# Two-layer fp32 backbone: weights, rows and accumulators moved to 0 modulo 512 bytes of SBUF

## The chip, the cores and the metric

The kernel runs on one core of a Trainium2 chip. The metric is the device time of one execution in microseconds (us). Below, PE is the matmul engine, PEld its weight loads (they run beside its matmuls), DVE the vector engine, ACT the scalar engine, POOL GpSimd and SP the engine that issues the DMAs.

## The reference

Two layers of a trunk work on 256 latent tokens and 256 context tokens, with D = 2048 and a hidden width of F = 5504, all in fp32. Layer 0 mixes tokens by pooling, on both streams. In layer 1 the latent tokens attend to a neighbourhood and to all context tokens (32 heads of 64), and the context is no longer written. A gated FFN with a width-3 convolution over tokens follows each mixer. The shift, scale and gate vectors of a layer come from `silu(c) @ w_mod`.

```python
def conv_ffn(u, w_gate, w_up, conv_w, conv_b, w_down):
    gp = jnp.pad(u @ w_gate, ((0, 0), (1, 1), (0, 0)))
    gte = gp[:, :T] * conv_w[0] + gp[:, 1:T + 1] * conv_w[1] + gp[:, 2:] * conv_w[2] + conv_b
    return (jax.nn.silu(gte) * (u @ w_up)) @ w_down
...
for i in range(DEPTH):
    ml = (silu_c @ w_mod[i] + b_mod[i]).reshape(B, 6, 1, D)
    mc = (silu_cc @ w_mod[i] + b_mod[i]).reshape(6, 1, 1, D)
    a_lat = modulate(rms_norm(h, norm1_g[i]), ml[:, 0], ml[:, 1])
    a_ctx = modulate(rms_norm(hc, norm1_g[i]), mc[0], mc[1])
    ... # y_lat, y_ctx: pool_mix in layer 0, neighbourhood_attention in layer 1
    h = h + ml[:, 2] * y_lat
    h = h + ml[:, 5] * conv_ffn(modulate(rms_norm(h, norm2_g[i]), ml[:, 3], ml[:, 4]), ...)
    if not last:
        hc = hc + mc[2] * y_ctx
        hc = hc + mc[5] * conv_ffn(modulate(rms_norm(hc, norm2_g[i]), mc[3], mc[4]), ...)
return rms_norm(h, final_norm_g)
```

## The kernel before

Activations are kept transposed: D runs over 16 tiles (KT) of 128 partitions, tokens along the free axis. `hl` and `hc` hold the two residual streams. A matmul streams token rows (the moving operand, 512 columns at a time) past a 128 by 128 weight block. Every fp32 operand is split into a high part, rounded to the fp32r format by a CAST on ACT, and a low part, the rest, subtracted on DVE. A product is then three matmuls: high by high, high by low, low by high. In layer 0 the 512 columns are the two streams side by side, and each k-tile takes the three matmuls in turn (`gu_mm`, L912 to L914, and `down0`, L949 to L951). In layer 1 high and low rows of the latent stream lie side by side, so that one matmul of 512 columns makes the first two products and one of 256 columns the third: eight of the one, then eight of the other (`gu_b`, L1102 and L1109; the o projection, L1466 and L1470), or four and four (`down1`, L1174 and L1178).

Weights arrive by SP's DMA queue as tiles of 128 x 1024 fp32 in the pool `wst` (4096 bytes per partition). `split` (L138) turns each tile, a half of a weight panel, into high and low tiles. It takes their buffers from a rotating list: the pool `whp` (three pairs) alone in most stages; in layer 0's FFN three turns of `whp` and one of `whx`; in layer 1's FFN three of `whp` and five of `whx1`. The normed rows lie in `ap0` (`A` in layer 0 and the projections, `oA` in layer 1), the activated hidden rows in the tiles `act` of the pool `f0` (layer 0) and `actb` of `f1` (layer 1).

Stages follow one another in the order norm and modulation, the pooling mixer with the first parts of the gate and up products (F-tiles 0 to 7), layer 0's FFN (`gu0(f)` for the gate and up products of F-tile f, `down0` once for every four F-tiles), attention, the o projection, layer 1's FFN (`gu1`, `down1`). The modulation for layer 1 is folded in among layer 0's FFN, on DVE and PE (L260, L282, `modt_b` at L320), and its sums are spread into `modT` (L330). `down0` evicts a PSUM bank on ACT (`dy`, L967) and adds it to `hl` and `hc` on POOL (L970).

SBUF tiles are placed by pools: a pool is opened where the last one ends, and the tiles of a pool stand in the order of their first mention, one address for all 128 partitions. A pool that is closed gives its space to the next ones, and an instruction on a new tile waits for what last used that space. A scheduler that is part of the build then puts the instructions of each engine in order by its own estimate of when each can run; so what a tile has to wait for can move an instruction. The pools `main`, `wst`, `whp` and `ap0` stay open throughout. Because `main` begins with the vector table `vt` of 3744 bytes, all that comes after it stands at other residues.

Residues modulo 512 bytes in the program as built, before: `wst`, `whp`, `ap0` and `hc` 192; `f0` (with `act`), `whx`, the modulation's sums and `whx1` 320; `f1` 192, with `actb` in it at 320; the attention's pools 448; `hl` 480.

Of the kernel before, what the change touches and what calls it, by code (L numbers as in the profile page):

```python
# [10 lines left out]
F32 = mybir.dt.float32  # L11
F32R = mybir.dt.float32r
# [5 lines left out]
P = 128  # L18
D = 2048
KT = D // P  # L20
T = 256
# [7 lines left out]
NK = BAND + T  # L29
# [3 lines left out]
NS = 8  # L33
# [27 lines left out]
def kernel(ctx: ExitStack, tc: tile.TileContext, xT, cxT, wmod, wg, wu, wd, wp,  # L61
                         wq, wv, wo, vec, cc, rope, inv, strips, out):
    nc = tc.nc
    main = ctx.enter_context(tc.tile_pool(name="main", bufs=1))
# [16 lines left out]
        return a.rearrange("p s t -> p (s t)")  # L81


    vt = main.tile([P, NVEC], F32, name="vt")
    nc.sync.dma_start(vt, vec)

# [1 line left out]
        a, b = _OFF[name]  # L88
        return vt[:, a:b]

    ones = main.tile([P, 1], F32, name="ones")
    nc.gpsimd.memset(ones, 1.0)
    minus_half = main.tile([P, 4], F32, name="minus_half")
    nc.gpsimd.memset(minus_half, -0.5)
    ident = main.tile([P, P], F32, name="ident")
    make_identity(nc, ident)

    sc2 = main.tile([P, KT, 2], F32, name="sc2")
    nc.sync.dma_start(sc2, cc)
    nc.scalar.activation(sc2, sc2, AF.Silu)  # L100
    hl = main.tile([P, KT, T], F32, name="hl")


    extra = []
# [367 lines left out]
    with ExitStack() as ph0:  # L472
        p0 = ph0.enter_context(tc.tile_pool(name="p0", bufs=1, reuse_waits="tile"))
# [9 lines left out]
            return f0.tile([P, 2, 512], dt, tag="act", bufs=7, name=name)  # L483

        PART = {}
        wsh = p0.tile([P, 2, NS, 2], F32, name="wsh")

        def late(f):

# [41 lines left out]

        with ExitStack() as phs:
            st = phs.enter_context(tc.tile_pool(name="st", bufs=2, reuse_waits="tile"))
            sc = st.tile([P, 32 * KT + 30], F32, bufs=1, name="sc")
            nc.gpsimd.memset(sc, 0.0)
            nc.vector.tensor_copy(sc[:, 30:].rearrange("p (k c) -> p k c", c=32)[:, :, 0:2], sc2)
# [7 lines left out]
                if 3 <= k < 13:  # L544
                    nc.tensor.matmul(warm[:, :T], ident, sq[:, :T], start=True, stop=True)
            pr = n1.rstd()
            rs1 = st.tile([P, 512], F32, bufs=1, name="rs1")
            nc.scalar.copy(rs1, pr)
            n2 = Norm(both, p0, "n2")
            n2.acc = p0.tile([P, 512], F32, name="n2acc")  # L550
# [4 lines left out]
            for j in range(2):  # L555
                t = st.tile([P, 2, WP], F32, bufs=1, name=f"pad{j}")
# [3 lines left out]
            for j in range(2):  # L560
                t = st.tile([P, 158], F32, bufs=1, name=f"sh{j}")
# [451 lines left out]
    for _ in moves:  # L1013
        pass
    tail, rows = _attention(tc, ap0, bank, ld, A, M, hl, wq, wv, wo, rope, band, ident, v_first)

    with ExitStack() as ph2:
        f1 = ph2.enter_context(tc.tile_pool(name="f1", bufs=8, reuse_waits="tile"))
# [11 lines left out]
        for k in range(KT):  # L1030
            a = raw[k] = rows[k][:, 1]
            with n4.urgent(k):
                nc.scalar.activation(a[:, 0], hl[:, k, :], AF.Copy, scale=M(1, 4, k, 0))
                nc.vector.scalar_tensor_tensor(a[:, 1], hl[:, k, :], M(1, 4, k, 0), a[:, 0].bitcast(F32),
                                               op0=ALU.mult, op1=ALU.subtract)
        sh = f1.tile([P, KT, 2], F32R, bufs=1, name="sh")
        for k in range(0, KT, 4):
            v = modT[1, 12 + k // 4][:, :, 0]
            nc.scalar.copy(sh[:, k : k + 4, 0], v)
# [215 lines left out]
def _attention(tc, ap0, bank, ld, A, M, hl, wq, wv, wo, rope, band, ident, v_first):  # L1255
# [9 lines left out]
    with ExitStack() as es:  # L1265
        op = es.enter_context(tc.tile_pool(name="op", bufs=1, reuse_waits="tile"))
        at = es.enter_context(tc.tile_pool(name="at", bufs=2, reuse_waits="tile"))
        rp = op.tile([P, 2, T], F32, name="rp")
        raw = at.tile([P, 2, T], F32, tag="sb", bufs=3, name="rope_rows")
        nc.sync.dma_start(raw, rope)  # L1270
# [2 lines left out]

        sts = []
        for j in range(2):
            t = op.tile([P, NK], F32, name=f"bias{j}")
            nc.gpsimd.memset(t, 0.0)
            sts.append(t)

        pts = []  # L1280
        for j in range(2):
            t = op.tile([P, 4, T], F32, name=f"pt{j}")
# [4 lines left out]
        for j in range(2):  # L1287
            t = op.tile([P, 2, T], F32R, name=f"qz{j}")
# [318 lines left out]
```

## Time and profile before

| | us |
|---|---|
| median of 3 runs | 3028.66 (3026.96 to 3032.0) |
| profiled execution, span | 3027.4 |
| layer 0's FFN, window 408 to 1664 | 1256.00 |
| attention up to the o projection, window 1664 to 2180 | 516.00 |
| layer 1's FFN, window 2289 to 3007 | 718.00 |

The profile is of one execution, and its span is 1.3 us below the median. A row of a window gives its length, then the busy time of each engine and the number of instructions in it, then the granted PE clock, the busy share of the DMA engines and what they moved. The durations that the profile gives to a matmul run to its end, which overlaps the next one; the time that a matmul costs in a row of many is the distance from start to start.

### The profile page before, as it was taken

How to read it: one execution, taken by the hardware profiler on the slowest of the kernel's cores; microseconds unless marked ns; L12 is line 12 of the kernel's file. 1: busy time of each engine (PE TensorE's matmuls, PEld its weight loads, DVE VectorE, ACT ScalarE, POOL GpSimd, SP SyncE). 2: the span in 40 equal slices, each digit the busy share in tenths (PEclk: the TensorE clock that was granted, in tenths of full speed). 3: DMA queues.
4: the chain of work that ended last, by engine and by line, in shares of the span. 5: the costliest groups of instructions: out<-in, count | busy, mean ns of one | idle time of the engine just before them, and what ended most of it. 6: DMA issues, size and time to landing. Idle time of an engine off the chain costs nothing.

```text
span 3027.4 us, 41070 instructions
## 1 busy us (share of the span) xinstructions
PE 2975.9 (98%) x14922; PEld 2405.5 (79%) x14922; DVE 2031.5 (67%) x2908; ACT 1353.1 (45%) x2225; POOL 872.1 (29%) x864
## 2 busy tenths in 40 slices
PE   7999999999999999999999999999999999999998
PEld 3655678887888888888887888888888888888887
DVE  4455887666776867687676666474777666666666
ACT  3333573323334233333334444343556666566665
POOL 1011310302214030332413111110101565566665
PEclk9999999999999999999999999999999999999999
DMA  9988535455865867786783333333356555555553
GB/s 380 342 299 324 197 99 179 159 170 167 251 201 186 257 178 234 210 234 200 216 241 101 115 108 114 99 110 108 112 162 206 175 196 194 188 182 188 182 187 112
DMA packets 224923, 572.32 MB, mean 189 GB/s; under 512 B 55248, under 2 KB 68304, under 8 KB 224720
## 3 DMA queue, kind: packets, MB, share of 16 engines
q1 hardware_dynamic: 224720, 569.70, 58.5%
q8 instruction: 117, 1.92, 0.3%
q14 instruction: 86, 0.70, 0.1%
HBM read 563.32 MB, written 11.53 MB: 190 GB/s over the span
## 4 chain that ended last, share of the span: by engine, by line
PE 89%; DVE 5%; DMA 2%; issue 1%; ACT 1%; SPq 0%; POOL 0%; POOLq 0%; DVEq 0%; ACTq 0%
PE u L1102 5%; PE g L1102 5%; PE d L1174 5%; PE d L949 5%; PE d L951 5%; PE d L950 5%; PE u L914 4%; PE u L912 4%; PE u L913 4%; PE g L914 4%; PE g L913 4%; PE g L912 4%; PE u L1109 3%; PE g L1109 3%; PE d L1178 3%; PE mod L195 2%
## 5 line engine op out<-in xcount | busy, mean ns | idle before, releaser
L970 POOL TENSOR_TENSOR hl<-hl,dy 128x256 f32<-128x256 f32 x144 | 145.1, 1008 | 943.4 <-ACT dy L967 678.4
L1191 POOL TENSOR_TENSOR hl<-hl,dy 128x256 f32<-128x256 f32 x320 | 313.5, 1011 | 234.4 <-ACT dy L1189 231.4
L282 DVE SCALAR_TENSOR_TENSOR macc<-wm,sc,macc 128x512 f32<-128x512 f32 x360 | 263.2, 780 | 8.1 <-DMA wm<-wmod 7.8
L260 DVE SCALAR_TENSOR_TENSOR macc<-wm,sc,macc 128x1024 f32<-128x1024 f32 x120 | 160.7, 1339 | 95.7 <-DMA wm<-wmod 94.5
L967 ACT ACTIVATE dy<-d,modT 128x256 f32<-128x256 f32 x224 | 93.2, 470 | 133.2 <-PE d L951 129.1
L970 POOL TENSOR_TENSOR hc<-hc,dy 128x256 f32<-128x256 f32 x144 | 141.9, 986 | 0.0
L1189 ACT ACTIVATE dy<-d,modT 128x512 f32<-128x512 f32 x160 | 104.5, 684 | 57.5 <-PE d L1178 57.2
L1371 POOL COPY bias<-rows 128x160 f32<-128x160 f32 x64 | 39.6, 628 | 311.6 <-DVE nm L1380 228.3
L153 DVE TENSOR_TENSOR wd_3l<-wd,wd_3h 128x1024 fp32r<-128x1024 f32 (+1 forms) x44 | 56.0, 1277 | 79.9 <-ACT wd_3h L150 79.9
L195 PE MATMUL mod<-wm,sc 128*32 128x512 f32 x640 | 96.5, 607 | 5.7 <-DMA wm<-wmod 5.5
L516 ACT ACTIVATE sg<-g 128x512 f32<-128x512 f32 x43 | 27.3, 634 | 153.2 <-DVE g L513 153.1
L153 DVE TENSOR_TENSOR wd_2l<-wd,wd_2h 128x1024 fp32r<-128x1024 f32 (+1 forms) x44 | 58.8, 1347 | 46.1 <-ACT wd_2h L150 46.1
L606 POOL TENSOR_TENSOR pf<-ws,inv 128x256 f32<-128x256 f32 x32 | 28.6, 914 | 196.6 <-DVE ws L598 137.6
L153 DVE TENSOR_TENSOR wd_1l<-wd,wd_1h 128x1024 fp32r<-128x1024 f32 (+1 forms) x44 | 55.3, 1260 | 37.7 <-ACT wd_1h L150 37.7
L150 ACT CAST wd_0h<-wd 128x1024 fp32r<-128x1024 f32 (+1 forms) x44 | 45.1, 1030 | 61.5 <-PE g L913 49.0
L150 ACT CAST wd_1h<-wd 128x1024 fp32r<-128x1024 f32 (+1 forms) x44 | 44.9, 1026 | 56.3 <-PE u L1102 29.6
L949 PE MATMUL d<-act,wd_0h 128*128 128x512 f32 x172 | 67.4, 395 | 1.0 <-ACT dy L967 1.0
L949 PE MATMUL d<-act,wd_3h 128*128 128x512 f32 x172 | 68.2, 396 | 0.0
L950 PE MATMUL d<-act,wd_2h 128*128 128x512 f32 x172 | 68.1, 396 | 0.0
L951 PE MATMUL d<-act,wd_1l 128*128 128x512 f32 x172 | 67.7, 394 | 0.2 <-DVE wd_1l L153 0.2
L951 PE MATMUL d<-act,wd_0l 128*128 128x512 f32 x172 | 67.9, 395 | 0.0
L949 PE MATMUL d<-act,wd_1h 128*128 128x512 f32 x172 | 67.9, 395 | 0.0
(1710 smaller groups left out, 9327.3 us busy)
## 6 DMA issues: line engine op xcount, KB each, us to landing
wm<-wmod SPq DMA_DIRECT2D x384, 512.0 KB, 6.2
wd<-wd SPq DMA_DIRECT2D x168, 512.0 KB, 4.4
wg<-wg SPq DMA_DIRECT2D x156, 512.0 KB, 4.4
wu<-wu SPq DMA_DIRECT2D x156, 512.0 KB, 4.7
wv<-wv SPq DMA_DIRECT2D x32, 512.0 KB, 3.9
wk<-wq SPq DMA_DIRECT2D x32, 512.0 KB, 3.9
wq<-wq SPq DMA_DIRECT2D x32, 512.0 KB, 3.7
wo<-wo SPq DMA_DIRECT2D x32, 512.0 KB, 4.4
```

Source lines behind the costliest of these rows:

```text
L153: low = eng.tensor_tensor(lo[:, :n], t[:, :n], hi[:, :n].bitcast(F32), op=ALU.subtract)
L282: nc.vector.scalar_tensor_tensor(acc[:, s], w, sc2[:, k, s : s + 1], acc[:, s], op0=ALU.mult, op1=ALU.add)
L912: nc.tensor.matmul(ps, hi[:, c : c + P], xh, start=(k == 0), stop=False)
L913: nc.tensor.matmul(ps, hi[:, c : c + P], xl, start=False, stop=False)
L914: nc.tensor.matmul(ps, lo[:, c : c + P], xh, start=False, stop=(k == KT - 1))
L949: nc.tensor.matmul(ps, hi[:, o : o + P], xh, start=(i == 0), stop=False)
L950: nc.tensor.matmul(ps, hi[:, o : o + P], xl, start=False, stop=False)
L951: nc.tensor.matmul(ps, lo[:, o : o + P], xh, start=False, stop=(i == n - 1))
L970: nc.gpsimd.tensor_tensor(h_of(s)[:, k, :], h_of(s)[:, k, :], y[:, s], op=ALU.add)
L1102: ins = nc.tensor.matmul(ps, hi[:, c : c + P], flat(x[k]), start=(k == 0), stop=False)
L1109: nc.tensor.matmul(ps[:, T:], lo[:, c : c + P], x[k][:, 0], start=False, stop=(k == KT - 1))
L1191: nc.gpsimd.tensor_tensor(hl[:, k, :], hl[:, k, :], y[:, q], op=ALU.add)
```

## The change

No operation, size or loop is changed, only where tiles stand. In `main`, `wsh` and `sh` come from other pools to the front, `sc2`, `ident` and `hl` ahead of `vt`, and `ones` is made 24 floats wide. In the pool `st`, `rs1` stands ahead of `sc`. The attention's two `bias` tiles go to a pool of their own, `odd`, opened behind the others.

```diff
@@ main pool
+    wsh = main.tile([P, 2, NS, 2], F32, name="wsh")
+    sh = main.tile([P, KT, 2], F32R, name="sh")
+    sc2 = main.tile([P, KT, 2], F32, name="sc2")
+    ident = main.tile([P, P], F32, name="ident")
+    hl = main.tile([P, KT, T], F32, name="hl")
     vt = main.tile([P, NVEC], F32, name="vt")
     nc.sync.dma_start(vt, vec)
...
-    ones = main.tile([P, 1], F32, name="ones")
+    ones = main.tile([P, 24], F32, name="ones")[:, 0:1]
     nc.gpsimd.memset(ones, 1.0)
     minus_half = main.tile([P, 4], F32, name="minus_half")
     nc.gpsimd.memset(minus_half, -0.5)
-    ident = main.tile([P, P], F32, name="ident")
     make_identity(nc, ident)
 
-    sc2 = main.tile([P, KT, 2], F32, name="sc2")
     nc.sync.dma_start(sc2, cc)
     nc.scalar.activation(sc2, sc2, AF.Silu)
-    hl = main.tile([P, KT, T], F32, name="hl")
@@ layer 0
         PART = {}
-        wsh = p0.tile([P, 2, NS, 2], F32, name="wsh")
...
             st = phs.enter_context(tc.tile_pool(name="st", bufs=2, reuse_waits="tile"))
+            rs1 = st.tile([P, 512], F32, bufs=1, name="rs1")
             sc = st.tile([P, 32 * KT + 30], F32, bufs=1, name="sc")
...
             pr = n1.rstd()
-            rs1 = st.tile([P, 512], F32, bufs=1, name="rs1")
             nc.scalar.copy(rs1, pr)
@@ layer 1
-        sh = f1.tile([P, KT, 2], F32R, bufs=1, name="sh")
         for k in range(0, KT, 4):
             v = modT[1, 12 + k // 4][:, :, 0]
             nc.scalar.copy(sh[:, k : k + 4, 0], v)
@@ attention
         op = es.enter_context(tc.tile_pool(name="op", bufs=1, reuse_waits="tile"))
         at = es.enter_context(tc.tile_pool(name="at", bufs=2, reuse_waits="tile"))
+        odd = es.enter_context(tc.tile_pool(name="odd", bufs=1, reuse_waits="tile"))
         rp = op.tile([P, 2, T], F32, name="rp")
...
-            t = op.tile([P, NK], F32, name=f"bias{j}")
+            t = odd.tile([P, NK], F32, name=f"bias{j}")
             nc.gpsimd.memset(t, 0.0)
             sts.append(t)
```

In the changed program as built, `wst`, `whp`, `ap0`, `hc`, `f0`, `act`, `whx`, the modulation's sums, `f1`, `actb`, `whx1`, `hl` and `ident` stand at 0 modulo 512, the attention's tiles at 0 and its score rows at 0 and 128, `vt` at 0, `sc2` and the second `bias` tile at 384. Every engine keeps its number of instructions, and lines stand one or two lower. `sh` and `bias` are in space that is free earlier, which moves a few instructions.

On POOL, before, behind the last adds of `down0` (`hl` and `hc` take `dy`, the first number being the output tile) and the norm (`n3v`), the two MEMSETs of `bias`:

```order
L970 TENSOR_TENSOR hl<-hl,dy_15_12756 128x256
L970 TENSOR_TENSOR hc<-hc,dy_15_12756 128x256
L388 TENSOR_TENSOR n3v_13076<-n3v_13076,minus_half 128x2
L388 TENSOR_TENSOR n3v_13080<-n3v_13080,minus_half 128x2
L1277 MEMSET bias_13478 128x416
L1277 MEMSET bias_13480 128x416
L1283 MEMSET pt_13482 128x1024
L1283 MEMSET pt_13484 128x1024
```

On POOL in the changed program, in the last but one pass of `down0`:

```order
L971 TENSOR_TENSOR hl<-hl,dy_11_12649 128x256
L971 TENSOR_TENSOR hc<-hc,dy_11_12649 128x256
L971 TENSOR_TENSOR hl<-hl,dy_12_12703 128x256
L971 TENSOR_TENSOR hc<-hc,dy_12_12703 128x256
L1278 MEMSET bias_13482 128x416
L1278 MEMSET bias_13484 128x416
L971 TENSOR_TENSOR hl<-hl,dy_13_12721 128x256
L971 TENSOR_TENSOR hc<-hc,dy_13_12721 128x256
L971 TENSOR_TENSOR hl<-hl,dy_14_12739 128x256
L971 TENSOR_TENSOR hc<-hc,dy_14_12739 128x256
```

The MEMSETs have moved up past the residual adds of three output tiles and past the norm.

On ACT, before, between attention and the o projection (`O` and `oA` are attention's output and its split, `wo3h` a cast weight):

```order
L1383 ACTIVATE sb_1_17920,sm_1_17923<-sb_1_17920,nm_1_17921 128x416
L1409 COPY O_17948<-o_17939 128x256
L1453 CAST oA_17957<-O_17948 128x256
L1039 CAST sh<-modT_86 128x4 x4
L150 CAST wo3h_18019<-wo_0_18015 128x1024
L150 CAST wo3h_18023<-wo_1024_18017 128x1024
```

On ACT in the changed program, in the last but one pass of `down0`:

```order
L152 CAST wd_10_0h_12770<-wd_10_0_1024_12764 128x512
L968 ACTIVATE dy_11_12649<-d_9_2_3_12636,modT_87 128x256 x2
L968 ACTIVATE dy_12_12703<-d_9_3_0_12690,modT_87 128x256 x2
L1039 CAST sh<-modT_88 128x4 x4
L968 ACTIVATE dy_13_12721<-d_9_3_1_12708,modT_87 128x256 x2
L968 ACTIVATE dy_14_12739<-d_9_3_2_12726,modT_87 128x256 x2
L152 CAST wd_10_1h_12841<-wd_10_1_0_12837 128x1024
```

The four casts of `sh` have moved up from the end of attention to the evictions of `down0`, and the four subtractions that follow them on DVE likewise.

On PE, before, in the o projection, at the third panel of `wo` (`h` is the high part, `l` the low part):

```order
L1466 MATMUL op_18027<-oA_17711,wo3h_18019 128x512
L1466 MATMUL op_18027<-oA_17714,wo3h_18019 128x512
L1466 MATMUL op_18074<-oA_17693,wo4h_18066 128x512
L1466 MATMUL op_18074<-oA_17696,wo4h_18066 128x512
L1466 MATMUL op_18074<-oA_17699,wo4h_18066 128x512
L1466 MATMUL op_18074<-oA_17702,wo4h_18066 128x512
L1466 MATMUL op_18074<-oA_17705,wo4h_18066 128x512
L1466 MATMUL op_18074<-oA_17708,wo4h_18066 128x512
L1470 MATMUL op_18027<-oA_17693,wo3l_18020 128x256
L1470 MATMUL op_18027<-oA_17696,wo3l_18020 128x256
```

On PE in the changed program, at the same place:

```order
L1467 MATMUL op_18031<-oA_17715,wo3h_18023 128x512
L1467 MATMUL op_18031<-oA_17718,wo3h_18023 128x512
L1471 MATMUL op_18031<-oA_17697,wo3l_18024 128x256
L1471 MATMUL op_18031<-oA_17700,wo3l_18024 128x256
L1471 MATMUL op_18031<-oA_17703,wo3l_18024 128x256
L1471 MATMUL op_18031<-oA_17706,wo3l_18024 128x256
L1471 MATMUL op_18031<-oA_17709,wo3l_18024 128x256
L1471 MATMUL op_18031<-oA_17712,wo3l_18024 128x256
L1471 MATMUL op_18031<-oA_17715,wo3l_18024 128x256
L1471 MATMUL op_18031<-oA_17718,wo3l_18024 128x256
```

The low products of the first half of `wo3` now stand ahead of the high products of `wo4`.

## Prediction

> **What bounds the kernel now.** I read the page's head first: the busy time of each engine, then the chain of work that ended last.
>
> ```profile
> PE 2975.9 (98%) x14922; PEld 2405.5 (79%) x14922; DVE 2031.5 (67%) x2908; ACT 1353.1 (45%) x2225; POOL 872.1 (29%) x864
> ...
> PE 89%; DVE 5%; DMA 2%; issue 1%; ACT 1%; SPq 0%; POOL 0%; POOLq 0%; DVEq 0%; ACTq 0%
> ```
>
> PE is busy for 98% of the span and makes 89% of the chain. No idle time of size is left, so a change of addresses matters only if a matmul itself gets quicker or slower. The windows by stage say where PE's time lies.
>
> ```profile
> core 0: us, PE busy (x) PEld busy (x) DVE busy (x) ACT busy (x) POOL busy (x), PEclk, DMA share, GB/s
> ...
> 408.00:1664.00 1256.00, 1250.45 (x5433) 1021.00 (x5434) 910.87 (x1118) 450.25 (x727) 281.14 (x290) 1.00 0.64 196
> 1664.00:2180.00 516.00, 516.00 (x2618) 425.29 (x2617) 318.83 (x697) 224.84 (x400) 67.56 (x99) 1.00 0.35 109
> 2289.00:3007.00 718.00, 716.71 (x4132) 629.12 (x4131) 463.02 (x515) 447.86 (x668) 429.09 (x366) 1.00 0.56 181
> ```
>
> The first row is layer 0's FFN (`gu0` and `down0` in turn), the second attention, the third layer 1's FFN. PE is never out of work and the clock is 1.00, yet time per matmul differs from stretch to stretch. A window cut at matmul starts shows it: its length over the count of weight loads (the number after PEld) is the spacing of starts.
>
> ```profile
> 500.27:505.86 5.59, 5.59 (x25) 4.53 (x24) 4.50 (x7) 2.36 (x4) 0.00 (x0) 1.00 0.32 97
> 505.86:522.20 16.34, 16.34 (x74) 13.52 (x72) 15.00 (x22) 3.68 (x5) 0.00 (x0) 1.00 0.54 166
> 422.88:434.07 11.19, 11.19 (x49) 9.01 (x48) 10.26 (x15) 7.78 (x15) 0.00 (x0) 1.00 0.35 96
> 436.86:438.23 1.37, 1.37 (x8) 1.13 (x6) 1.37 (x3) 1.37 (x6) 0.00 (x0) 1.00 0.03 12
> 1705.91:1716.79 10.88, 10.88 (x49) 9.01 (x48) 3.60 (x3) 2.62 (x4) 0.00 (x0) 1.00 0.49 146
> ```
>
> All are 512-column fp32r matmuls. In `gu0`, 24 in 5.59 us are 232.9 ns each, and the next 72, in the same pass, 16.34/72 = 226.9. In `down0` 48 in 11.19 us are 233.1 ns and a run of 6 is 1.37/6 = 228. The k projection of attention runs at 10.88/48 = 226.7. Neither DVE's load nor DMA's explains this (the quick 72 have the busier DVE and DMA). Placement does: in the program as built, `A` and the pool `whp` start at 192 modulo 512 bytes of a partition, while `act`, `actb` and the pools `whx` and `whx1` start at 320. The slow 24 of `gu0` take weights from `whx` against rows in `A` (320 against 192), the quick 72 from `whp` (192, 192). In `down0` the rows lie in `act`: `whp` weights (192 against 320) are slow and `whx` (320, 320) quick. So four pairings fall into two speeds: **equal residues lock near 226.8 ns, unequal ones drift near 233.** That both equal pairs are quick, at two different residues, is why I read it as a matter of the difference and not of the residue itself.
>
> **The change part by part.** Every pool and tile that feeds a matmul's rows or its weights goes to 0 modulo 512. What was equal stays equal; what was unequal becomes equal.
>
> ```profile
> 845.22:932.97 87.75, 87.75 (x385) 72.17 (x384) 73.08 (x87) 22.72 (x27) 1.44 (x2) 1.00 0.81 239
> 533.24:577.77 44.53, 44.53 (x194) 36.11 (x192) 14.75 (x16) 18.43 (x40) 25.72 (x30) 1.00 0.37 121
> L949 PE MATMUL d<-act,wd_0h 128*128 128x512 f32 x172 | 67.4, 395 | 1.0 <-ACT dy L967 1.0
> ```
>
> `gu0`: four whole F-tiles are 384 matmuls in 87.75 us, 228.5 each; this is 3/4 of 226.9 and 1/4 of 232.9 (228.4), as one weight half in four lies in `whx`. It runs 35 tiles (8 to 42) of 96, 3360 matmuls: 3360 x (228.5 - 226.9) = **5.4 us**. `down0`: one pass is 192 in 44.53 us, 231.9 each; twelve groups of 172 like the one shown are 2064: 2064 x (231.9 - 226.9) = **10.3 us**.
>
> ```profile
> 2224.23:2274.51 50.28, 50.28 (x291) 44.26 (x289) 37.41 (x58) 26.51 (x38) 0.00 (x0) 1.00 0.62 194
> 2335.33:2377.36 42.03, 42.03 (x242) 36.81 (x241) 29.16 (x34) 22.34 (x35) 9.61 (x4) 1.00 0.61 187
> 2447.45:2455.86 8.41, 8.41 (x50) 7.35 (x49) 5.28 (x7) 6.22 (x12) 3.43 (x5) 1.00 0.33 124
> ```
>
> Layer 1 alternates 8 matmuls of 512 columns with 8 of 256. The o projection, all equal now, takes 50.28/18 = 2.793 us for such a block; `gu1`, where five weight halves of eight are unequal, 42.03/15 = 2.802. It has 43 x 2 x 2 = 172 blocks: 172 x 0.009 = **1.5 us**. `down1` in blocks of 4 and 4 takes 8.41/6 = 1.402 us where rows and weights agree already, against 2.793/2 = 1.397: between 0 and 160 x 0.005 = 0.9 us, and I take **0**, as agreeing pairs are what the change would give it. Attention, the v projection and the partial gate products read `A` by `whp`: equal before and after, 0.
>
> The other engines: POOL's residual adds show what residues do off PE.
>
> ```profile
> L970 POOL TENSOR_TENSOR hl<-hl,dy 128x256 f32<-128x256 f32 x144 | 145.1, 1008 | 943.4 <-ACT dy L967 678.4
> ...
> L970 POOL TENSOR_TENSOR hc<-hc,dy 128x256 f32<-128x256 f32 x144 | 141.9, 986 | 0.0
> ```
>
> The same add is 1008 ns on `hl` (480 modulo 512) and 986 on `hc` (192); even 22 ns on each of 144 would be 3 us of an engine that is 29% busy, all behind PE: 0. For DMA the two ends are these.
>
> ```profile
> 30.00:60.00 30.00, 24.82 (x97) 8.15 (x95) 15.55 (x30) 7.85 (x15) 6.15 (x8) 0.94 1.03 407
> ...
> PE mod L195 <- DMA wm<-wmod: 5.5, 8, 1.7
> PE op L1466 <- DVE oA L1454: 2.9, 2, 1.6
> ```
>
> At the start the queue moves 407 GB/s into staging tiles at residue 192 with its engines full, and PE waits for `wm` 5.5 us in all. If aligned tiles landed quicker, at most those 5.5 us go; if slower, the same share of the opening is added, another 5.5 or so. I take 0, for later stages need 109 to 239 GB/s of that 407.
>
> **What moves in time.** `bias` no longer waits for `op`'s old space, and `sh` no longer for `f1`, so both are made earlier, late in `down0`.
>
> ```profile
> 1612.97 0.59 PE L320 MATMUL modt_b<-modr,quad 128*128 128x256 f32 x2
> 1614.92 0.18 DVE L330 SCALAR_TENSOR_TENSOR modT<-modT,vt 128x16 f32<-128x16 f32 x1
> 1616.45 0.84 ACT L967 ACTIVATE dy<-d,modT 128x256 f32<-128x256 f32 x2 [5.72 <-PE d L951]
> 1617.00 0.74 POOL L970 TENSOR_TENSOR hl<-hl,dy 128x256 f32<-128x256 f32 x1 [5.13 <-ACT dy L967]
> 2207.70 0.47 ACT L1039 CAST sh<-modT 128x4 fp32r<-128x4 f32 x4
> 2208.17 0.37 DVE L1040 TENSOR_TENSOR sh<-modT,sh 128x4 fp32r<-128x4 f32 x4
> L1277 POOL MEMSET bias<- x2: 445/446/447, 1685.4 to 1685.8; 128x416 f32 x2
> ```
>
> The two MEMSETs (2 x 446 ns) now stand on POOL ahead of `dy_13`'s adds and wait for the fold of the modulation (`modt_b`, over at 1613.6). POOL was idle for 5.13 us until 1617.00, so they fit. Behind them are only residual adds, with most of a pass to spare. ACT's four CASTs of `sh` (0.47 us) come ahead of `dy_13`'s eviction and wait for DVE's spread at 1615.1; ACT was idle for 5.72 us until 1616.45, so they end near 1615.6. If that spread came 1 us later, the eviction and the PSUM bank behind it would slip 0.5 us, which the spare banks take. DVE loses 0.37 us at 2208.17, where PE did wait for it: a gain of at most 0.4. On PE, `wo3`'s low products now run ahead of `wo4`'s first six high ones and need DVE's subtraction about 1.4 us sooner (6 x 0.227): between -0.4 and +1.4 us, taken at 0.
>
> **Sum:** 5.4 + 10.3 + 1.5 = 17.2 us from the profiled execution's span of 3027.4. The median is 3028.7, 1.3 more than that span, so 3028.7 - 17.2 = 3011.5. DVE is busy for 73.08 of 87.75 us in `gu0`; a quicker PE will now and then wait there, and I allow half a microsecond: **3012 us**. Its own range is 3003 (all at 226.7, the 5.5 us of DMA and 2 of small moves gained) to 3020 (half the gain).
>
> **The rivals.** *Nothing happens* (0.17): the drift comes from something that goes with these buffers, such as how far apart they lie, or that the two pools of a pass alternate. Against it: the four pairings above change partner and speed together. It gives 3025 to 3032, about 3028. The Trainium skill speaks for it: "SBUF — State Buffer", section "Who interferes with whom", gives PE two independent read ports, one for the moving rows and one for the weights, and says that PE never waits on anyone; by that rule the sum is 0. The trace disagrees as far as 226.9 and 232.9 ns lie in one pass, with the same clock and less DVE and DMA work in the slow part.
>
> *The fixed part goes too* (0.08): if 0 modulo 512 is special. An 8 and 8 block of 2.793 us with 226.7 for 512 columns leaves (2793 - 8 x 226.7)/8 = 122.4 for 256, so 2 x 122.4 - 226.7 = 18 ns of each matmul don't grow with columns. The program has about 13,200 of them: half of it gone is 13,200 x 9 = 119 us, near 2893 with the 17 above. Against it: 192 and 320 lock at the same spacing. By the skill's "TensorE: Matmul & The Clock Gate", section "Back-to-back issue gap", a lone gap is N/2.4 + 2.5, about 216 ns at 512 columns; 10.7 ns on 10,432 of these would be an estimated 112 us. No stretch of this trace shows 216.
>
> *It locks at the slow end* (0.08). Starts in drift pass through better and worse positions.
>
> ```profile
> L949 PE MATMUL d<-act,wd_2h x172: 390/392/404, 445.2 to 1644.0; 128*128 128x512 f32 x172
> ```
>
> Between the shortest and the longest lie 14 ns. If with rows and weights both at 0 the two streams meet in the worst position, and stay there, spacing is 226.9 + 14 = 240.9: in `gu0` 3360 x 12.4 = 42 us and in `down0` 2064 x 9.0 = 19 us more, and some 3000 matmuls in stages that are equal now lose 14 ns each, 42 more: 3028.7 + 103 = about 3131, slower. It decides at the present mean of the two, (3360 x 228.5 + 2064 x 231.9)/5424 = 229.8 ns. Against it: both equal pairs found the quick end.
>
> **How the numbers follow.** The forecast has 0.67. What a measurement can tell from no change here is about 0.2%, 6 us, so 3022.6 and 3034.7 are the bounds. Faster: 0.67 and 0.08 make 0.75; the same 0.17; slower 0.08. The range from 3000 to 3032 takes in the forecast with its unknown costs and the case of no change, 0.84; the two far cases stay outside.
>
> **What would show it.** Windows cut in the same way: in the changed kernel every stretch of `gu0` and `down0` at 226.7 to 227, four F-tiles in 87.1 us instead of 87.75, a whole `down0` pass in 43.6 instead of 44.53, a block of `gu1` in 2.793. Stages that agree now (the k projection, the o projection) should keep 226.7 and 2.793; if they move, the residue itself matters, and the forecast fails on its main step. If `down0` keeps 231.9, addresses are not the cause. If spacing falls as forecast and the time doesn't, the waits of PE for DVE will have grown.

## The result and the profile after

The changed kernel takes 3011.15 us (median of 4 runs, 3006.95 to 3012.74) against 3028.71 before (4 runs): a ratio of 0.9935, with a 95% interval of 0.9921 to 0.9949. It is faster, by 17.6 us; the forecast was 3012 us.

The profile's windows over the same matmuls as in the prediction, now of the changed kernel (again length, busy time and count of PE, PEld, DVE, ACT and POOL, then clock, DMA share and GB/s):

```profile
core 0: us, PE busy (x) PEld busy (x) DVE busy (x) ACT busy (x) POOL busy (x), PEclk, DMA share, GB/s
420.15:431.03 10.88, 10.88 (x50) 9.01 (x48) 10.17 (x15) 7.69 (x15) 0.00 (x0) 1.00 0.32 99
...
496.31:501.75 5.44, 5.44 (x26) 4.50 (x24) 4.35 (x7) 2.37 (x4) 0.00 (x0) 1.00 0.33 99
501.75:518.07 16.32, 16.32 (x74) 13.51 (x72) 14.54 (x22) 3.79 (x5) 0.00 (x0) 1.00 0.53 161
528.95:572.47 43.52, 43.52 (x194) 36.04 (x192) 17.03 (x18) 18.41 (x40) 26.73 (x30) 1.00 0.39 132
836.48:923.52 87.04, 87.04 (x385) 72.07 (x384) 73.20 (x87) 22.85 (x28) 1.44 (x2) 1.00 0.82 241
1686.07:1696.95 10.88, 10.88 (x49) 9.01 (x48) 3.60 (x3) 2.61 (x4) 0.00 (x0) 1.00 0.46 146
2204.28:2254.56 50.28, 50.28 (x291) 44.24 (x289) 37.43 (x58) 26.51 (x38) 0.00 (x0) 1.00 0.60 190
2315.18:2357.08 41.90, 41.90 (x242) 36.88 (x241) 29.17 (x34) 22.36 (x35) 9.62 (x4) 1.00 0.62 189
2427.00:2435.42 8.42, 8.42 (x50) 7.36 (x49) 5.28 (x7) 6.22 (x12) 3.42 (x5) 1.00 0.37 125
```

The slow 24 of `gu0` now take 5.44 us, 226.7 ns each, the same as the 72 behind them (16.32/72). The 48 of `down0` are down from 11.19 to 10.88 us. Four F-tiles of `gu0` take 87.04 us and a pass of `down0` 43.52: 384 and 192 times 226.7. The stretches that agreed before, the k and the o projection, keep 10.88 and 50.28 us. Fifteen blocks of `gu1` (a block is the eight matmuls of 512 columns and the eight of 256 behind them) went from 42.03 to 41.90, which is 2.793 us each, and `down1`'s six blocks kept 8.4.

Where each stage begins and ends is read from the first and last start of a group of matmuls. The view lists for a line and tile the durations (min, median, max in ns) and the first and last start. Before:

```profile
L912 PE MATMUL g<-A,wg_8h x16: 389/389/497, 396.6 to 419.5; 128*128 128x512 f32 x16
L951 PE MATMUL d<-act,wd_3l x172: 389/393/398, 456.8 to 1652.8; 128*128 128x512 f32 x172
L1102 PE MATMUL g<-oA,wg_0h x24: 389/396/481, 2277.5 to 2300.1; 128*128 128x512 f32 x24
L1178 PE MATMUL d<-actb,wd_3l x160: 274/281/290, 2402.6 to 2997.0; 128*128 128x256 f32 x160
```

The changed kernel (L912 and L951 of before are L913 and L952 there; the lines of layer 1's FFN keep their numbers):

```profile
L913 PE MATMUL g<-A,wg_8h x16: 388/389/501, 394.0 to 416.7; 128*128 128x512 f32 x16
L952 PE MATMUL d<-act,wd_3l x172: 388/389/397, 453.2 to 1632.7; 128*128 128x512 f32 x172
L1102 PE MATMUL g<-oA,wg_0h x24: 388/396/486, 2257.6 to 2280.0; 128*128 128x512 f32 x24
L1178 PE MATMUL d<-actb,wd_3l x160: 277/280/283, 2382.3 to 2975.2; 128*128 128x256 f32 x160
```

Layer 0's FFN went from 1652.8 - 396.6 = 1256.2 us to 1632.7 - 394.0 = 1238.7, **17.5 less**. Attention with the o projection stayed (624.7 and 624.9 us). Layer 1's FFN went from 719.5 to 717.6, **1.9 less**. The span fell by 22.2 us; the rest is 2.6 us in the opening and 0.4 behind the last of these matmuls. The opening is scatter, as a second profile of the same kernel shows below. (By these rows layer 0's FFN begins 11 us ahead of the window that the prediction called by that name; no term of it rests on that window.)

The schedule's moves landed where there was room. In the timeline of the changed kernel (start, duration, engine, and in brackets the idle time ahead of it):

```profile
1593.74 0.59 PE L322 MATMUL modt_b<-modr,quad 128*128 128x256 f32 x2
1594.39 0.83 POOL L1278 MEMSET bias<- 128x416 f32 x2 [1.76 <-PE modt_b L322]
1594.73 0.92 DVE L328 TENSOR_TENSOR modT<-modt_b,vt 32x64 f32<-32x64 f32 x4
1595.68 0.48 ACT L1039 CAST sh<-modT 128x4 fp32r<-128x4 f32 x4 [4.18 <-DVE modT L328]
1597.17 0.84 ACT L968 ACTIVATE dy<-d,modT 128x256 f32<-128x256 f32 x2 [1.01 <-PE d L952]
```

ACT ends the four casts at 1596.16 and still waits 1.01 us for PE before the next eviction.

### The profile page after: what moved, and what is told of

It is laid out like the page before. It is cut to its first block, busy times and chain, and to the rows that moved or that the text cites. A ratio compares the mean times of both kernels' runs of the same rounds, so it can differ in the third digit from the quotient of the medians.

```text
span 3005.2 us, 41071 instructions
## 1 busy us (share of the span) xinstructions
PE 2954.4 (98%) x14922; PEld 2402.8 (80%) x14922; DVE 2035.4 (68%) x2908; ACT 1353.9 (45%) x2225; POOL 876.8 (29%) x864
## 4 chain that ended last, share of the span: by engine, by line
PE 93%; DVE 3%; DMA 2%; ACT 1%; issue 1%; POOL 0%; SPq 0%; DVEq 0%; ACTq 0%; POOLq 0%
PE g L1102 5%; PE u L1102 5%; PE d L950 5%; PE d L952 5%; PE d L951 5%; PE d L1174 5%; PE u L915 4%; PE u L913 4%; PE u L914 4%; PE g L915 4%; PE g L914 4%; PE g L913 4%; PE u L1109 3%; PE g L1109 3%; PE d L1178 3%; PE mod L197 2%
## 5 line engine op out<-in xcount | busy, mean ns | idle before, releaser
L1191 POOL TENSOR_TENSOR hl<-hl,dy 128x256 f32<-128x256 f32 x320 | 313.6, 1011 | 231.6 <-ACT dy L1189 228.7
L968 ACT ACTIVATE dy<-d,modT 128x256 f32<-128x256 f32 x224 | 93.2, 470 | 121.0 <-PE d L952 114.9
L952 PE MATMUL d<-act,wd_2l 128*128 128x512 f32 x172 | 67.2, 390 | 0.0
L951 PE MATMUL d<-act,wd_2h 128*128 128x512 f32 x172 | 67.1, 390 | 0.0
L950 PE MATMUL d<-act,wd_2h 128*128 128x512 f32 x172 | 66.9, 389 | 0.0
L952 PE MATMUL d<-act,wd_0l 128*128 128x512 f32 x172 | 66.9, 389 | 0.0
```

The costliest lines, as they stand in the source:

```text
L950: nc.tensor.matmul(ps, hi[:, o : o + P], xh, start=(i == 0), stop=False)
L951: nc.tensor.matmul(ps, hi[:, o : o + P], xl, start=False, stop=False)
L952: nc.tensor.matmul(ps, lo[:, o : o + P], xh, start=False, stop=(i == n - 1))
L1191: nc.gpsimd.tensor_tensor(hl[:, k, :], hl[:, k, :], y[:, q], op=ALU.add)
```

## The experiments

The theory: PE's spacing is set by the difference between the addresses of the moving rows and of the weights, and by nothing else in the change. The rivals: 0 modulo 512 is itself what counts; or the gain comes from the moved instructions and small tiles. Each kernel below keeps every engine's order of instructions as in the kernel before (the first) or as in the changed kernel (all others); only addresses differ.

### All at 192, old order

```diff
-        wsh = p0.tile([P, 2, NS, 2], F32, name="wsh")
+        wsh = p0.tile([P, 8, NS, 2], F32, name="wsh")[:, 0:2]
-        sh = f1.tile([P, KT, 2], F32R, bufs=1, name="sh")
+        sh = f1.tile([P, 4 * KT, 2], F32R, bufs=1, name="sh")[:, 0:KT]
```

> Order of tiles and every engine's order of instructions as in the kernel before; only act, actb, whx and whx1 are moved by 128 or 384 bytes, so that rows and weights all stand at 192 modulo 512. Theory 1 (only the difference between rows and weights counts): gu0 and down0 lock at 226.6 to 226.9 ns a matmul, four F-tiles take 87.1 us, and the time is that of the changed kernel, 3008 to 3014 us (ratio 0.9935). Theory 2 (0 modulo 512 is what counts): down0 keeps 231.9 or so and the time stays at 3028. Theory 3 (the gain is from bias and sh being made earlier, or from the DMA of aligned tiles): no gain here, 3028, and the opening up to the first partial product at 86 us as before.

It takes 3009.33 us (median of 5 runs), ratio to the kernel before 0.9939 (0.9926 to 0.9951). Four F-tiles, a pass of `down0` and fifteen blocks of `gu1`:

```profile
838.54:925.58 87.04, 87.04 (x386) 72.07 (x385) 73.10 (x87) 24.11 (x29) 1.44 (x2) 1.00 0.82 243
530.66:574.18 43.52, 43.52 (x194) 36.04 (x192) 15.52 (x17) 18.45 (x40) 25.32 (x30) 1.00 0.38 126
2316.27:2358.17 41.90, 41.90 (x243) 36.88 (x242) 29.18 (x34) 22.36 (x35) 9.61 (x4) 1.00 0.61 188
```

87.04, 43.52 and 41.90 us: the changed kernel's numbers to the last digit, with no rows and no weights at 0. Theory 1 holds. Two tiles made wider do the whole work of the change. (The first partial product starts at 73.9 us here and at 74.7 before; the expectation's 86 us does not fit either.)

### Old residues, new order

```diff
-    minus_half = main.tile([P, 4], F32, name="minus_half")
+    minus_half = main.tile([P, 52], F32, name="minus_half")[:, 0:4]
-            n2.acc = p0.tile([P, 512], F32, name="n2acc")
+            n2.acc = p0.tile([P, 544], F32, name="n2acc")[:, 0:512]
+        f1.tile([P, 32], F32, bufs=1, name="fill")
```

> Order of tiles and every engine's order of instructions as in the changed kernel; whp, ap0 and hc stand at 192 again and act, actb, whx and whx1 at 320. Theory 1 (only the difference counts): gu0 back at 228.5 ns and down0 at 231.9, time 3027 to 3031 us, ratio 1.000. Theory 3 (the gain comes with the moved instructions, or with hl, ident and sc2 at their new places): stays at 3008 to 3014.

3027.79 us (11 runs), ratio 0.9995 (0.9986 to 1.0004). The same three windows:

```profile
843.46:931.21 87.75, 87.75 (x385) 72.15 (x384) 73.19 (x87) 23.14 (x28) 1.43 (x2) 1.00 0.81 241
532.29:576.82 44.53, 44.53 (x194) 36.12 (x192) 15.76 (x17) 18.43 (x40) 25.51 (x30) 1.00 0.37 122
2333.15:2375.18 42.03, 42.03 (x242) 36.80 (x241) 29.21 (x34) 22.35 (x35) 9.61 (x4) 1.00 0.61 188
```

These are the numbers of before. The new order of tiles and instructions, and `hl` and `ident` at 0, are worth nothing that can be measured: at most some 4 us by the interval.

### Which differences matter

Three kernels keep all weights at 0 and put the rows of `gu0` (`A`) and those of `down0` (`act`) at other residues, by unused tiles ahead of them. For 64 and 256 (the other two have other sizes at the same places):

```diff
+    ap0.tile([P, 16], F32, name="fill_rows")
-            n2.acc = p0.tile([P, 512], F32, name="n2acc")
+            n2.acc = p0.tile([P, 560], F32, name="n2acc")[:, 0:512]
+        whx.tile([P, 64], F32, name="fill_whx")
+        f1.tile([P, 48], F32, bufs=1, name="fill_f1")
+        whx.tile([P, 64], F32, bufs=1, name="fill_whx1")
```

> The changed kernel with all weights at 0 modulo 512, rows A at 64 and act and actb at 256, one difference in each stage. Theory 1a (any difference drifts): gu0 and down0 both at 231 to 233.5 ns, so 3360 x 5.5 = 18 us and 2064 x 5.5 = 11 us over the changed kernel, about 3040, and layer 1 slower by 2 to 4 us. Theory 1b (it goes by a period shorter than 512 bytes, 64 or 256): the stage whose difference is a multiple of that period locks at 226.7; with 256, down0 locks and gu0 doesn't, 3029; with 64 both lock, 3011.

> The changed kernel with weights at 0, A at 32 and act and actb at 192. Theory 1a (any difference drifts): both stages at 231 to 233.5 ns, about 3040 us. Theory 1b with a period of 64 bytes: down0 locks at 226.7, gu0 doesn't, about 3029. Theory 1c (the difference matters by its size): gu0 at 32 bytes still locks, near 226.7 to 228, and down0 drifts at 232 to 233, about 3023.

> The changed kernel with all weights at 0, A at 320 and act and actb at 352 modulo 512. If the pattern repeats every 256 bytes (as 256 apart locked like 0), 320 must act like 64: gu0 in a cycle of three, 231.6, 226.1 and 229.2 ns, mean 229.0, and down0 at 96 drift near 233; time 3014.6 + 2064 x 6.2 = 3027 us. If only 0 and 256 are special and the rest is plain drift, or the period is 512: gu0 at 232 to 233.5 ns, 13 us more, near 3041.

One run each: 3014.57, 3054.79 and 3028.62 us. Four F-tiles of `gu0` and a pass of `down0`, rows 64 and 256 above the weights:

```profile
839.37:927.28 87.91, 87.91 (x386) 72.12 (x384) 73.12 (x87) 23.01 (x28) 1.44 (x2) 1.00 0.81 240
530.27:573.84 43.57, 43.57 (x193) 36.04 (x192) 14.64 (x16) 18.43 (x40) 25.69 (x30) 1.00 0.38 123
```

32 and 192 above:

```profile
855.10:944.69 89.59, 89.59 (x386) 71.97 (x384) 73.18 (x86) 22.83 (x28) 1.42 (x2) 1.00 0.79 236
539.10:583.74 44.64, 44.64 (x194) 36.01 (x193) 14.40 (x15) 18.39 (x40) 25.63 (x30) 1.00 0.36 117
```

320 and 352 above:

```profile
845.04:932.94 87.90, 87.90 (x385) 72.11 (x384) 73.09 (x87) 23.98 (x29) 1.44 (x2) 1.00 0.80 243
532.85:577.64 44.79, 44.79 (x194) 36.06 (x192) 14.75 (x16) 18.42 (x40) 25.69 (x30) 1.00 0.35 120
```

Divided by 384 and 192, the spacing by difference (rows less weights; 0 is the changed kernel, 128 the slow 48 of `down0` before, 11.19/48) is

| difference, bytes | 0 | 32 | 64 | 128 | 192 | 256 | 320 | 352 |
|---|---|---|---|---|---|---|---|---|
| ns a matmul | 226.7 | 233.3 | 228.9 | 233.1 | 232.5 | 226.9 | 228.9 | 233.3 |

Theory 1a (any difference drifts) falls: 256 locks as 0 does, and 320 acts as 64. What these points bear out is a **period of 256 bytes**, not 512. The slow 24 of `gu0` before fit in: their rows stand 128 below their weights, which is 128 above modulo 256, and they took 232.9 ns. At 64 and 320 there is a steady cycle: by the records' starts, spacings of about 232, 226 and 229 ns follow one another in turn (at 64 the three matmuls of a k-tile have means of 231.6, 226.1 and 229.2). 1c falls too: 32, the smallest difference, is among the worst. The run with 32 and 192 also shows the slow side: placed badly, the program takes 44 us more than the changed kernel with every engine's instructions in the same order, and 26 more than the kernel before.

Two of the three times were not as expected. Theory 1b had 3029 us for a period of 256, with 64 as slow as the rest; 64 costs only 2.2 ns a matmul, and the time was 3014.57. At 320 and 352 it came out as a period of 256 has it, 3028.62 against 3027. At 32 and 192 it was 3054.79 where 1a had about 3040: layer 0's FFN is 35.1 us longer than in the changed kernel, where 29 was reckoned, and attention with the o projection, whose rows are off by 32 too, 7.6 longer.

The sign counts. In the v projection the weights of the model are the moving operand and `A` is loaded into the array, so the first of these kernels has its moving operand 64 below what is loaded:

```profile
1653.86:1676.25 22.39, 22.39 (x97) 18.05 (x96) 22.39 (x47) 13.63 (x24) 1.95 (x3) 1.00 0.21 71
```

96 in 22.39 us are 233.2 ns, where the same kernel's `gu0` had 228.9. DVE is busy all through, but so it is over the same 96 in the changed kernel, which take 227.5 ns each:

```profile
1645.20:1667.03 21.84, 21.84 (x97) 18.04 (x96) 21.84 (x46) 13.41 (x24) 1.52 (x2) 1.00 0.21 73
```

With a period of 256, 64 below is the same as 192 above, and 192 is a slow place for long runs of 512 columns.

### A version that uses it

With the rows 64 above, `gu1` was faster than in the changed kernel although `gu0` was slower (fifteen blocks, against 41.90 us in the changed kernel's row above):

```profile
2326.98:2368.31 41.33, 41.33 (x242) 36.39 (x241) 29.27 (x34) 22.30 (x35) 9.66 (x4) 1.00 0.61 191
```

In blocks of eight matmuls of 512 and eight of 256 columns, equal addresses lose the lock at each change of shape. By the records' starts, every one of the changed kernel's 135 blocks that run without a break goes the same way: 233, 236, 228, 233 and 231 ns, then 227 three times, and 113, 119 and six times 120 for the 256 columns. That is 2793.3 ns a block (standard deviation 0.5). With the rows 64 above there is no such start: the 135 blocks take 2764.2 on average, 29 ns less, most of it in the matmuls of 256 columns (116.1 ns against 119.1). The fifteen of the row above are among the better ones, 38 less, and the expectations below reckon with 26. Since `whp` and the rows are shared with layer 0, only layer 1's own buffers can be moved: `whx1` to 64 below the rows, and `actb`.

```diff
+        f1.tile([P, 48], F32, bufs=1, name="fill_f1")
+        whx.tile([P, 64], F32, bufs=1, name="fill_whx1")
```

> The changed kernel, with layer 1's extra weight buffers whx1 64 bytes below the rows oA (448 against 0 modulo 512) and actb at 192; layer 0 and attention are untouched. From the run with rows 64 above weights: five weight halves of eight in gu1 go from 8 x (230.3 + 119.05) to 8 x (229.9 + 116.2) ns, 5/8 x 172 x 26 ns = 2.8 us less; down1 from 350.2 ns a pair to a mixture of 347.4 (192 apart) and 349.95 (256 apart), 640 x 1.2 ns = 0.8 us less. Theory 1 (spacing is set by the difference alone): layer 1's FFN 3 to 4 us shorter than in the changed kernel, 3005 to 3009 us. Rival (the gain at 64 needs all eight halves at that difference, each change of buffer starting the drift again): gu1 within 1 us of the changed kernel, 3010.

The second kernel has a fill of 16 floats in `f1` in their place:

> As the last, but whx1 at 64 (weights 64 above the rows) and actb at 64. Theory 1, sign does not matter: gu1 like the last run, 2 to 3 us shorter than the changed kernel. Theory 2, the sign matters: gu1 at or above the changed kernel's 8 x (230.3 + 119.05) ns a block. down1 is 64 apart in three halves of eight and equal in five: near 350 ns a pair.

The first takes 3004.49 us (5 runs), ratio 0.9922 (0.9908 to 0.9935); the second, with `whx1` above the rows, 3007.11 (one run). Fifteen blocks of `gu1` in the first:

```profile
2317.41:2358.94 41.53, 41.53 (x243) 36.61 (x241) 29.28 (x34) 22.35 (x35) 9.67 (x4) 1.00 0.60 190
```

and in the second:

```profile
2318.07:2359.78 41.71, 41.71 (x242) 36.50 (x241) 29.25 (x34) 22.35 (x35) 9.60 (x4) 1.00 0.59 189
```

41.53 against 41.90 is 25 ns a block in these fifteen. Over all 135 it is 20.5 (2772.8 against 2793.3), 3.5 us in 172, where 2.8 was expected: blocks on `whx1` went to 2762.8, and those on `whp`, which stay equal, to 2789.4, so these gain a little too. So the gain doesn't need all eight halves, and the rival falls. The 0.8 us expected of `down1` did not come: its 123 blocks without a break take 1400.3 ns on average, as in the changed kernel. In the second kernel the 135 blocks take 2782.2 ns, 11 less, 1.9 us: about half of what the rows above the weights give, and neither of that run's theories. The blocks on `whx1`, there 192 above modulo 256, take 2776.0: in alternating shapes 192 is quicker than 0, unlike in long runs of 512 columns. The last pair sets the changed kernel beside the version with `actb` at 128:

```diff
-        f1.tile([P, 48], F32, bufs=1, name="fill_f1")
-        whx.tile([P, 64], F32, bufs=1, name="fill_whx1")
+        f1.tile([P, 32], F32, bufs=1, name="fill_f1")
+        whx.tile([P, 80], F32, bufs=1, name="fill_whx1")
```

> The changed kernel itself, for its time beside the next one on the same chip. 3009 to 3013 us; gu0 and down0 at 226.7 ns as in its first profile; if the 3 us that its first profile saved up to the first partial product come from alignment they are there again (71.7 us), if they are scatter that stretch lies anywhere from 71.5 to 74.7.

> The version with whx1 at 448 (64 below the rows of gu1), with actb at 128 instead of 192: down1 then has its rows 192 above five weight halves of eight (347.4 ns for a 512 and a 256 column matmul, as measured at 192) and 128 above three (350.9 or a little more), mean 348.7, against 349.9 for the version with actb at 192: 640 x 1.2 ns = 0.8 us less, so 3003 to 3006 us, 6 to 7 below the changed kernel. Rival (the short runs of four and four don't keep to these means): down1 within 0.3 us or slower.

The changed kernel took 3009.29 us (3007.66 to 3011.88), ratio 0.9935 (0.9922 to 0.9947). The version took 3004.37 (3003.81 to 3005.73), ratio 0.9919 (0.9906 to 0.9933). Their five runs each on the same chip don't overlap: **4.9 us faster than the changed kernel**, and the lowest median here (6 to 7 were expected). Its layer 1 FFN runs from 2259.3 to 2972.4, 713.1 us, against 717.6:

```profile
L1104 PE MATMUL g<-oA,wg_0h x24: 388/394/483, 2259.3 to 2281.2; 128*128 128x512 f32 x24
L1180 PE MATMUL d<-actb,wd_3l x160: 274/281/287, 2382.7 to 2972.4; 128*128 128x256 f32 x160
```

That `actb` is better at 128 than at 192 can't be told from the times, 3004.37 and 3004.49 us; by the starts a block of `down1` takes 1397.5 ns against 1400.3, 0.4 us over 160 where 0.8 was expected.

The opening settles itself with the second profile of the changed kernel. One group of the partial products (its first start is the first time behind the durations) before, in the changed kernel and in its repetition:

```profile
L786 PE MATMUL cg<-Ad,wcg_4h x64: 387/394/499, 114.9 to 381.1; 128*128 128x512 f32 x64
```

```profile
L787 PE MATMUL cg<-Ad,wcg_4h x64: 387/396/499, 112.4 to 378.5; 128*128 128x512 f32 x64
```

```profile
L787 PE MATMUL cg<-Ad,wcg_4h x64: 387/395/499, 114.0 to 380.0; 128*128 128x512 f32 x64
```

114.9, 112.4 and 114.0 us: one and the same kernel differs by 1.6 us here, most of the 2.5 by which its first profile was ahead. The same start lies at 114.1 and 114.0 us in the two kernels whose staging tiles are at 192 (all at 192, and old residues with the new order), and at 115.3 in the first of the two kernels that move `whx1`, whose staging tiles are at 0. No run shows a gain for DMA from aligned tiles.

## Why the prediction was right

- **`gu0` and `down0`**: the step was right. The prediction gave 5.4 and 10.3 us, 15.7 together; layer 0's FFN lost 17.5. The locked value is 226.7, not 226.9: the stretch of 72 from which 226.9 was read still held the relock behind the slow 24, 16.34 us against 16.32 now. At 226.7 the terms are 3360 x 1.8 = 6.0 and 2064 x 5.2 = 10.7 us. The 0.8 us that are left lie within the scatter between profiles: the same stage takes 1239.0 us in the repetition and 1240.0 with all at 192, and 1254.8 with the old residues against 1256.2 before.
- **`gu1`**: 2.793 us a block was forecast and measured; 1.5 us was the term, and the FFN of layer 1 lost 1.9. One part of the step was not right: what was equal did not stay as it was. By the starts, blocks on `whx1` went from 2808.1 to 2793.3 ns, and blocks on `whp`, equal before and after, rose from 2788.7 to 2793.3. The sum hardly notices (7.5 ns a block over the 135, 1.3 us in 172).
- **`down1`** was taken at 0 from a stretch where rows and weights agreed already, and its six blocks kept 8.4 us. Three weight halves of eight did not agree (`actb` at 320, `whp` at 192), and over the 123 blocks that run without a break the mean went from 1403.2 to 1400.3 ns, 0.5 us in 160: inside the 0 to 0.9 us given.
- **The equal stages** were taken at 0, and the k and o projections kept 10.88 and 50.28 us.
- **DMA, POOL and the moved instructions** were taken at 0 with bounds. With old residues and the new order the time is that of before, within 0.9986 to 1.0004. Half a microsecond was allowed for PE waiting on DVE; those waits add up to 15.3 us before and to 15.2 and 16.9 in the two profiles of the changed kernel, so nothing can be told of it. The reading that POOL's adds take their time from the residues of `hl` and `hc` was wrong: with both where they were before and other tiles moved (all at 192), the adds take 966 and 1035 ns, where they took 1008 and 986.
- **The rival of no change** is out: with the order kept and the rows moved to 32 above the weights, PE's spacing in `gu0` goes from 226.7 to 233.3 ns. The Trainium skill ("SBUF — State Buffer", section "Who interferes with whom") speaks for that rival, since PE's two read ports are said to be independent; if that means that their addresses don't matter to each other, the measurement disagrees.
- **The fixed part** stayed: equal residues at 0 give the same 226.7 as at 192. The 216 ns at 512 columns that the Trainium skill gives for a lone matmul ("TensorE: Matmul & The Clock Gate", section "Back-to-back issue gap") is shown by no run here.
- **The slow end** at equal residues did not come; slow places exist, at other differences.

That 3012 lies within 1 us of the median is partly luck: the changed kernel's second median is 3009.29, and each median is of runs 4 to 6 us apart.

That addresses set the spacing is shown. How they do it is not: that the reading of the moving rows collides with the loading of the next weights is argued from the difference of the two addresses being what counts. No experiment took the weight load away, the profile gives a weight load 187 to 188 ns in quick and slow stretches alike (72.07 and 71.97 us for 384, at 0 and at 32), and why the period is 256 bytes is open.

## What to carry to other kernels

Where PE is busy all the time and matmuls of one shape show two spacings, compare the addresses of moving rows and loaded weights modulo 256 bytes before looking at other engines: here 0 or 256 apart was best for long runs of 512 columns, and rows 64 above the weights for blocks of eight of 512 and eight of 256. A few filler floats ahead of a pool set the difference; absolute alignment isn't needed. Any edit that changes the size of an early small tile can move all pools behind it. The placements tried here lie 50 us apart (3004.37 to 3054.79), so control for addresses when a harmless edit gets a verdict.

## What was not expected

The period is 256 bytes where the change aligns to 512. A difference of 32 bytes costs as much as any (233.3 ns). At 64 the spacing isn't uniform but cycles by three, with one matmul in three at 226.1 ns, below the locked 226.7. For alternating shapes 64 is better than 0, by 29 ns a block, 23 of them in the matmuls of 256 columns. And the timing is exact: the same windows in kernels with different orders and absolute addresses agree to 0.01 us in 87.
